# Row scaling by a diagonal matrix inside the transposes, and memory values computed token-major, in a one-core streaming encoder layer

## The chip, the cores and the metric

The kernel runs on one core of one Trainium2 chip. The metric is device time in microseconds (us). The core has TensorE (PE in the profile; PEld is its weight load), VectorE (DVE), ScalarE (ACT), GpSimd (POOL) and SyncE (SP), which here issues every DMA.

## The reference

One layer of an encoder, in float32, for 1024 prompt rows and 64 sample rows of width 1024. Only its beginning matters here:

```
h  = rmsnorm(x, g_pre)                 # x * rsqrt(mean(x*x) + eps) * g, row by row
... = split(h @ w_in)                  # 1024 -> 9216 columns: q, k, v, u, sv, mq, gates
kv = rmsnorm(mem, g_mem) @ w_mem_kv    # 256 memory tokens, 1024 -> 2048 columns
mem_k, mem_v = split(kv)               # each (256 tokens, 4 heads, 256); both are outputs
```

Then come stick-breaking attention, a spatial gating unit, attention over the memory, a gated merge, an output projection and a SwiGLU feed-forward, all fed by these products.

## The kernel before

**Precision and products.** A float32 operand is split into a high part (a cast to a reduced type, `Xh...`, `memh`, the first half of `whl`) and a low part (`Xl...`, `meml`: operand minus high part), and each product of the code (`mm3`, line 248) is three TensorE instructions: high by high, high by low, low by high.

**Memory stage.** The two 128-row memory tiles `mt` get their sum of squares on ScalarE (`rms_stage`, output `junk`), `rstd` from VectorE and GpSimd, a scaling by `rstd` in place (`scale_stage`), eight transposes of 128x128 each on TensorE (`tr4`, line 702, into the PSUM tiles `pt`, of which there are two), a scaling by the columns of g in the evacuation (`gain`, line 713: one VectorE instruction of 512 columns, or four ScalarE instructions of 128), and the split into `memh` and `meml`. Then `memkv_pair` (line 812) does w_mem_kv in eight pairs: for each of four heads 256 columns of k, then 256 of v. A pair loads two pieces `raw` of 512 KB, splits each into two `whl` (128x512), and multiplies: with each `whl` 12 TensorE instructions of 256 columns, called a chunk below, so 4 chunks a pair and 32 in all. The weights stand as the stationary operand, so the result has the output columns on its partitions (`mkT`, evacuated by ScalarE), and four transposes turn each pair back (`pt`, copied to `mko` by VectorE, stored).

**The x tiles.** Nine row tiles `xt` (eight of 128 rows, one of 64) go the same way: load, squares on ScalarE, `rstd`, scaling in place, `tr4`, `gain` into `bt`. `form_stages` (line 731) then makes the eight right-hand sides of a Strassen-type product from them: B11, B21, B22 are splits of `bt`; T2, T1, T3, T4 are sums and differences first, and then splits (f1 to f7). T2 and T1 need two subtractions on VectorE each, and one subtraction runs on GpSimd (`psub`).

**What sets the order.** The engines execute a fixed order, which the Python code writes out. It keeps its own model of each engine's clock (`Clocks`, line 93), and holds the x work as streams: lists of stages, each with the engine and a function that says when it is ready. Between and inside the chunks, `breathe` and `fill` take stages from the streams:

```
def breathe():
    tick()
    while clock["dve"] < clock["pe"] + BACK[0] and clock["act"] < clock["pe"] + BACK[0]:
        st = ready(0)
        if st is None:
            break
        go(st)
```

`ready` takes a stage whose operand is ready by the later of TensorE's and the stage's engine's modelled clock; BACK is 6 in the memory stage. `lighter` and `gain` choose between VectorE and ScalarE by these clocks. Nearly all instructions are recorded by one helper, line 83, so groups are told by tile names. After the memory stage the 36 Strassen units over w_in start, with `XhB11a` as the first right-hand side.

Of the kernel before, what the change touches and what calls it, by code (L numbers as in the profile page):

```python
# [9 lines left out]
F32 = mybir.dt.float32  # L10
F32R = mybir.dt.float32r
AF = mybir.ActivationFunctionType
ALU = mybir.AluOpType
AX = mybir.AxisListType

P = 128
T = 1088
HT = 544
D = 1024
# [73 lines left out]
class Clocks:  # L93
# [43 lines left out]
    def at(self, *tiles):  # L137
        return max([self.wrote.get(x.tensor.name, (0,))[0] for x in tiles], default=0) + self.LATENCY
# [16 lines left out]
def encoder_layer(  # L155
# [14 lines left out]
    clock, at = clocks.t, clocks.at  # L170
    nc = Engines(tc.nc, clocks)
# [3 lines left out]
    sm = ctx.enter_context(tc.tile_pool(name="sm", bufs=4))  # L175
# [6 lines left out]
    def nm(s):  # L182
        cnt[0] += 1
        return f"{s}_{cnt[0]}"

    def A(shape, dt=F32, s="a"):
        return arena.tile(shape, dt, tag="s", name=nm(s), bufs=NSLOT)

    def U(shape, dt=F32, s="u"):
        return arena.tile(shape, dt, tag="u", name=nm(s), bufs=NSMALL)  # L190
# [3 lines left out]
    def PB():  # L194
        t = ps.tile([P, 1024], F32, tag="b", name=nm("pb"), bufs=3)
        banks["b"] = banks["b"][-2:] + [t]
        return t
# [6 lines left out]
    def psum_free(tag, n=1):  # L204

        h = banks[tag]
        return clocks.done(h[n - 1]) if len(h) == (3 if tag == "b" else 2) else 0
# [3 lines left out]
    def f32(ap):  # L211
        return ap.bitcast(F32)
# [7 lines left out]
    def store(dst, src):  # L220
        nc.sync.dma_start(dst, src)

    def act(out, in_, f=AF.Copy, **kw):
        nc.scalar.activation(out, in_, f, **kw)
# [10 lines left out]
    def lighter(src, n, cost_dve):  # L235

        t = at(src)
        return max(clock["dve"], t) + cost_dve < max(clock["act"], t) + 0.1 + 0.00084 * n

    def split(src, hi, lo):  # L240
        n = math.prod(list(src.shape)[1:])
        if src.space == bass.MemoryType.SB and lighter(src, n, DVE_BIAS + 0.07 + 0.00057 * n):
            nc.vector.tensor_copy(hi, src)
        else:
            act(hi, src)
        sub(lo, src, f32(hi))

    def mm3(out, wh, wl, xh, xl, start, stop):
        nc.tensor.matmul(out, lhsT=wh, rhs=xh, start=start, stop=False)
        nc.tensor.matmul(out, lhsT=wh, rhs=xl, start=False, stop=False)  # L250
        nc.tensor.matmul(out, lhsT=wl, rhs=xh, start=False, stop=stop)

    def tp(out, in_):
        n = in_.shape[0]
        nc.tensor.transpose(out, in_, ident[:n, :n])


    ident = keep.tile([P, P], F32, tag="ident", name="ident")
# [13 lines left out]
    memk = [dtile([P, 1024], f"memk{h}") for h in range(4)]  # L272
    memv = [dtile([P, 1024], f"memv{h}") for h in range(4)]
# [24 lines left out]
    def later(n, fn, src=()):  # L298
        due.append((max([clock[e] for e in ("pe", "act", "dve")]) + 2.5 * n if n else at(*src), fn))
# [10 lines left out]
    def stream(*stages):  # L310
        st = list(stages)
        streams.append(st)
        return st
# [41 lines left out]
# [9 lines that stand above are left out]
    def fill(t):  # L364

        while clock["pe"] < t - 0.2:
            st = ready(t - 0.2)
# [3 lines that stand above are left out]
# [23 lines left out]
    def get_raw(i):  # L394
        return raw_t[i]
# [33 lines left out]
    def wop(fn, *rs):  # L429

        wops.append(fn)
        for r in rs:
            first_wop.setdefault(r, len(wops) - 1)
            last_wop[r] = len(wops) - 1
        return len(wops) - 1
# [12 lines left out]
    def raw_load(srcs, nk):  # L448

        def f():  # L450
            r = A([P, nk, 256], F32, "raw")
            w = 256 // len(srcs)
            for i, s in enumerate(srcs):
                load(r[:, :, i * w:(i + 1) * w], s.rearrange("(k p) m -> p k m", p=P))
            return r
        raws.append(f)
        return len(raws) - 1
# [216 lines left out]
    def rms_stage(x, d, junk=None):  # L674
# [7 lines left out]
            d["r"] = rstd_of(ss, D)  # L682
        return ("act", lambda: at(x()), sq)

    def scale_stage(get):

        def need():
            d = get()
            return None if d is None else at(d["r"])

        def sc():
            d = get()
            x, o = d["x"], d.pop("j")
            if lighter(x, D, 0.07 + 0.00057 * D):
                nc.vector.tensor_scalar(o, x, d["r"], None, op0=ALU.mult)
            else:
                act(o, x, scale=d["r"])
            d["x"] = o
            d["scaled"] = True
        return ("act", need, sc)  # L700

    def tr4(d):

        src = d["x"]
        n = src.shape[0]
        for h in range(2):
            pt = PT().rearrange("p (k q) -> p k q", k=4)
            for k in range(4):
                tp(pt[:, k, :n], src[:, (4 * h + k) * P:(4 * h + k + 1) * P])
            yield slice(4 * h, 4 * h + 4), pt[:, :, :n]  # L710
        d.clear()

# [96 lines left out]

    MH = {}  # L810

    def memkv_pair(h, kv):
        col = kv * D + h * 256
        parts = [([w_mem_kv[0, kh * 512:(kh + 1) * 512, col:col + 256]], 4) for kh in range(2)]
        st = {}

        def evac(m, hi, pt):
            if m == 0:
                st["t"] = U([P, 2, 256], F32, "mkT")
            act(st["t"][:, m, :], pt[:, :256])  # L820
            if m == 1:
                stream(("pe", lambda: max(at(st["t"]), psum_free("t")), fin))

        def fin():
            t = st["t"]
            pt = PT().rearrange("p (m d) -> p m d", m=2)
            for m in range(2):
                for dt in range(2):
                    tp(pt[:, m, dt * P:(dt + 1) * P], t[:, dt, m * P:(m + 1) * P])
            o = U([P, 2, 256], F32, "mko")  # L830
            nc.vector.tensor_copy(o, pt)
            dst = mem_v_prompt if kv else mem_k_prompt

            hl = A([P, 2, 2, 256], F32R, "mhl")
            split(o if kv else t, hl[:, 0], hl[:, 1])

            def put():
                store(dst[0, 0, :, h, :].rearrange("(m p) d -> p m d", p=P), o)
                store((memv if kv else memk)[h], f32(hl).rearrange("p s m d -> p (s m d)"))
            later(0, put, (o, hl))  # L840
        conv_pair(parts, lambda k, t, s: (MH["h"][k // 4][:, k % 4, :], MH["l"][k // 4][:, k % 4, :]),
                  [[(0, "a", cols_of(0, 256))]], evac)

    for h in range(4):
        for kv in range(2):
            memkv_pair(h, kv)
    n_mem = len(steps)


# [1196 lines left out]
    r = 0  # L2046
# [156 lines left out]
```

## Time and profile before

| | |
|---|---|
| median of 3 runs | 2277.43 us (2275.89 to 2277.76) |
| the profiled execution | 2276.9 us, of which its span 2275.2 us |
| PE busy | 2215.2 us, 97% of the span, 16465 matmul records |
| DVE busy | 1545.1 us, 68% |
| ACT busy | 756.6 us, 33% |
| mean granted TensorE clock | 0.994 |
| HBM read, written | 234.86 MB, 131.80 MB |

Shares over the whole span hide the beginning, in which the engines are loaded otherwise than later; the table by stretches below is read for that. A line of the timeline gives the start, the duration of the merged run of instructions, the engine, what is written and read, and in brackets how long the engine had been idle and what ended that. Consecutive instructions overlap in their pipelines, so the cost of one in a stream is the distance of two starts, which is less than its duration.

### The profile page before, as it was taken

The numbers are of one execution on the slowest core, as the hardware profiler recorded it, in microseconds if no ns is written. First come the engines' busy times: TensorE is split into PE (matmuls) and PEld (weight loads), VectorE is DVE, ScalarE is ACT, GpSimd is POOL, SyncE is SP. The second block draws the span as 40 slices with busy tenths as digits, with TensorE's granted clock in tenths as the row PEclk, the third lists the DMA queues.
The fourth block names the chain that finished last, engine by engine and source line by source line (L and its number), as shares of the span: only waits on it lengthen the run. The fifth ranks groups of instructions, "written<-read, shape, count | busy, mean of one in ns | idle before, by whom it ended". The sixth has DMA issues, their size and how long they took to land. (4 is left out here: it accounts for less than half of the span.)

```text
span 2275.2 us, 40734 instructions
## 1 busy us (share of the span) xinstructions
PE 2215.2 (97%) x16465; PEld 2141.9 (94%) x16465; DVE 1545.1 (68%) x2433; ACT 756.6 (33%) x1390; POOL 95.2 (4%) x172
## 2 busy tenths in 40 slices
PE   7899999999999999999999999997999999999998
PEld 6899999999999999889999999997999999998876
DVE  7955688865777776788734343458677677675677
ACT  8442222232212232566522021344112112124353
POOL 2000000000000000011000000121000000000000
PEclk9999999999999999999999999998999999999999
DMA  6523355775476658876835252132332233257235
GB/s 209 186 87 106 123 208 199 236 221 162 171 260 217 220 187 268 296 294 219 281 123 165 88 164 68 60 104 74 91 118 89 78 118 93 74 179 261 84 112 185
DMA packets 288367, 368.27 MB, mean 162 GB/s; under 512 B 20628, under 2 KB 220404, under 8 KB 288180
## 3 DMA queue, kind: packets, MB, share of 16 engines
q1 hardware_dynamic: 288180, 365.67, 48.6%
q8 instruction: 130, 2.13, 0.4%
q14 instruction: 57, 0.47, 0.1%
HBM read 234.86 MB, written 131.80 MB: 161 GB/s over the span
## 5 line engine op out<-in xcount | busy, mean ns | idle before, releaser
L83 ACT ACTIVATE whl<-raw 128x512 fp32r<-128x512 f32 x250 | 154.4, 633 | 519.8 <-PE pb L83 200.2
L83 DVE TENSOR_TENSOR c<-pb,u 128x544 f32<-128x544 f32 (+2 forms) x236 | 168.3, 713 | 230.4 <-PE pb L83 218.2
L83 PE MATMUL pb<-fop,fop 128*128 128x512 f32 x924 | 219.2, 390 | 1.9 <-DVE p L83 1.6
L83 PEld LDWEIGHTS pb<-fop,fop 128*128 128x128 f32 x924 | 173.0, 188 | 40.5 <-DVE p L83 2.4
L83 DVE TENSOR_TENSOR whl<-raw,whl 128x512 fp32r<-128x512 f32 x270 | 181.3, 686 | 12.5 <-ACT whl L83 11.8
L83 DVE TENSOR_TENSOR u<-pb,u 128x544 f32<-128x544 f32 (+2 forms) x177 | 125.7, 710 | 57.5 <-PE pb L83 56.6
L83 DVE TENSOR_TENSOR whl<-u,whl 128x512 fp32r<-128x512 f32 x232 | 160.1, 690 | 6.0
L83 PE MATMUL pb<-XhB11a,whl 128*128 128x288 f32 x592 | 130.8, 296 | 0.2 <-DVE whl L83 0.2
L83 PE MATMUL pb<-XhB21a,whl 128*128 128x288 f32 x592 | 130.8, 296 | 0.0
L83 PE MATMUL pb<-XhB22a,whl 128*128 128x288 f32 x592 | 130.3, 295 | 0.3 <-DVE whl L83 0.2
L83 PE MATMUL pb<-XhB11b,whl 128*128 128x256 f32 x592 | 119.8, 285 | 0.0
L83 ACT ACTIVATE c<-c 128x1088 f32<-128x1088 f32 x38 | 42.4, 1115 | 232.8 <-DVE c L83 232.8
L83 PE MATMUL pb<-XhB21b,whl 128*128 128x256 f32 x592 | 118.7, 283 | 0.0
L83 PE MATMUL pb<-XhB22b,whl 128*128 128x256 f32 x592 | 118.6, 283 | 0.0
L83 PE MATMUL pb<-XhT2a,whl 128*128 128x288 f32 x464 | 104.4, 300 | 2.7 <-DVE whl L83 0.6
L83 PE MATMUL pb<-XhT1a,whl 128*128 128x288 f32 x464 | 102.0, 295 | 1.0 <-DVE sgo L83 1.0
L83 PE MATMUL pb<-XhT3a,whl 128*128 128x288 f32 x464 | 102.2, 296 | 0.0
L83 PE MATMUL pb<-Xrh,whl 128*128 128x288 f32 (+1 forms) x512 | 100.0, 291 | 2.3 <-ACT ysq L83 2.3
L83 PE MATMUL pb<-XhT4a,whl 128*128 128x288 f32 x464 | 102.0, 295 | 0.0
L83 PEld LDWEIGHTS pb<-XhB22a,whl 128*128 128x128 f32 x592 | 99.0, 188 | 0.8 <-DVE whl L83 0.8
L83 PEld LDWEIGHTS pb<-XhB11a,whl 128*128 128x128 f32 x592 | 99.0, 188 | 0.7 <-DVE whl L83 0.4
L83 PEld LDWEIGHTS pb<-XhB21a,whl 128*128 128x128 f32 x592 | 99.0, 188 | 0.0
(330 smaller groups left out, 6247.4 us busy)
## 6 DMA issues: line engine op xcount, KB each, us to landing
raw<-in_w_in_dram SPq DMA_DIRECT2D x72, 512.0 KB
raw<-in_w_ffn_in_dram SPq DMA_DIRECT2D x88, 256.0 KB
gsc<-c SPq DMA_DIRECT2D x24, 544.0 KB
grow<-gsc SPq DMA_DIRECT2D x24, 544.0 KB
raw<-in_w_branch_dram SPq DMA_DIRECT2D x24, 512.0 KB
fS<-fsum SPq DMA_DIRECT2D x44, 256.0 KB
fw<-in_w_ffn_out_dram SPq DMA_DIRECT2D x44, 256.0 KB
fa<-fS SPq DMA_DIRECT2D x44, 256.0 KB
```

What stands on the lines that cost most here:

```text
L83: r = fn(*a, **k)
```

## The change

Two things. First, a tile that was to be scaled in place (the memory tiles and the nine x tiles; not the rows of the feed-forward, whose scaling has another target) is not scaled any more. Instead VectorE writes a 128x128 `diag` (the identity times `rstd`), and `tr4` multiplies the tile, as stationary operand, by it: an ordinary float32 product in the place of a transpose. At most three diags are open at a time. Second, the value half of `memkv_pair` becomes `memv_pair`: the memory tokens are the stationary operand and the weights the moving one, so that the result has tokens on its partitions and is evacuated to `mko` by ScalarE, without the transposes, `mkT` and the copy.

```
     def scale_stage(get):
         def need():
             d = get()
-            return None if d is None else at(d["r"])
+            return None if d is None or d["j"] is d["x"] and DIAG[0] == 3 else at(d["r"])
         def sc():
             d = get()
             x, o = d["x"], d.pop("j")
-            if lighter(x, D, 0.07 + 0.00057 * D):
+            if o is x:
+                DIAG[0] += 1
+                n = x.shape[0]
+                g = d["g"] = sm.tile([P, P], F32, tag="diag", name=nm("diag"), bufs=3)[:n, :n]
+                nc.vector.tensor_scalar(g, ident[:n, :n], d["r"], None, op0=ALU.mult)
+            elif lighter(x, D, 0.07 + 0.00057 * D):
                 nc.vector.tensor_scalar(o, x, d["r"], None, op0=ALU.mult)
...
             for k in range(4):
-                tp(pt[:, k, :n], src[:, (4 * h + k) * P:(4 * h + k + 1) * P])
+                a = src[:, (4 * h + k) * P:(4 * h + k + 1) * P]
+                if g is None:
+                    tp(pt[:, k, :n], a)
+                else:
+                    nc.tensor.matmul(pt[:, k, :n], lhsT=a, rhs=g, start=True, stop=True)
+            if g is not None and h == 1:
+                DIAG[0] -= 1
...
+    def memv_pair(h):
...
+            def f(tiles, kh=kh):
+                if kh == 0:
+                    fill(psum_free("b"))
+                    st["p"] = PB()
+                for q, w in enumerate(tiles):
+                    fill(at(w, MH["h"][kh], MH["l"][kh]))
+                    for m in range(2):
+                        for k in range(2):
+                            sl = (slice(None), 2 * q + k, slice(m * P, m * P + P))
+                            mm3(st["p"][:, m * 512:m * 512 + 256], MH["h"][kh][sl], MH["l"][kh][sl],
+                                w[:, 0, k], w[:, 1, k], kh == q == k == 0, kh == q == k == 1)
+                    breathe()
+                if kh == 1:
+                    st["o"] = U([P, 2, 256], F32, "mko")
+                    act(st["o"], st.pop("p").rearrange("p (m n) -> p m n", m=2)[:, :, :256])
+                    stream(("dve", lambda: at(st["o"]), fin))
+                    breathe()
```

Since the order comes out of the modelled clocks, it changes too, up to the first Strassen unit; from there on every engine's order is as before. Two places matter.

TensorE, from the last memory transposes (`mt`) to the x tiles (`xt`); `pb` is the accumulator of a pair. Before:

```order
L83 MATMUL pt_359<-ident,mt_299 128x128 x4
L83 MATMUL pb_388<-memh_314,whl_374 128x256
...
L83 MATMUL pb_388<-memh_315,whl_377 128x256
...
L83 MATMUL pb_455<-memh_314,whl_380 128x256
...
L83 MATMUL pb_455<-memh_315,whl_385 128x256
...
L83 MATMUL pt_493<-ident,xt_389 128x128 x4
L83 MATMUL pt_499<-ident,xt_389 128x128 x4
L83 MATMUL pb_491<-memh_314,whl_449 128x256
...
L83 MATMUL pt_554<-ident,xt_399 128x128 x4
```

And now:

```order
L83 MATMUL pt_361<-diag_332,mt_299 128x128 x4
L83 MATMUL pb_385<-memh_314,whl_373 128x256
...
L83 MATMUL pt_433<-diag_430,xt_386 128x128 x4
L83 MATMUL pt_439<-diag_430,xt_386 128x128 x4
L83 MATMUL pt_467<-diag_464,xt_394 128x128 x4
L83 MATMUL pt_473<-diag_464,xt_394 128x128 x4
L83 MATMUL pt_488<-diag_454,xt_402 128x128 x4
...
L83 MATMUL pt_626<-diag_623,xt_553 128x128 x4
L83 MATMUL pt_632<-diag_623,xt_553 128x128 x4
L83 MATMUL pb_385<-memh_315,whl_376 128x256
```

Before, the x tiles stood one by one between memory chunks, the first after four chunks; now all nine stand between the first chunk and the second.

VectorE, around the first x tiles (`diag` and `xt` are the scalings, `bt<-pt,cols` the evacuations by `gain`, `whl` the low parts of memory weights). Before:

```order
L83 TENSOR_SCALAR xt_389<-xt_389,rstd_394 128x1024
L83 CAST whl_449<-raw_372 128x512
L83 TENSOR_TENSOR whl_449<-raw_372,whl_449 128x512
L83 TENSOR_TENSOR whl_452<-raw_383,whl_452 128x512
L83 TENSOR_TENSOR whl_483<-raw_372,whl_483 128x512
L83 TENSOR_TENSOR whl_488<-raw_383,whl_488 128x512
L83 TENSOR_TENSOR bt_55_492<-pt_493,cols 128x512
L83 TENSOR_SCALAR rstd_526<-ss_59_523 64x1
L83 TENSOR_TENSOR XlB11a_530<-bt_55_492,XhB11a_529 128x4x128
```

And now:

```order
L83 TENSOR_SCALAR diag_430<-ident,rstd_391 128x128
L83 TENSOR_TENSOR bt_48_432<-pt_433,cols 128x512
L83 TENSOR_TENSOR bt_48_432<-pt_439,cols 128x512
L83 TENSOR_SCALAR rstd_451<-ss_52_448 64x1
L83 TENSOR_SCALAR diag_454<-ident,rstd_421 128x128
L83 CAST XhB11a_456<-bt_48_432 128x4x128
L83 TENSOR_TENSOR XlB11a_457<-bt_48_432,XhB11a_456 128x4x128
L83 TENSOR_TENSOR XlB21a_461<-bt_48_432,XhB21a_460 128x4x128
L83 TENSOR_SCALAR diag_464<-ident,rstd_399 128x128
L83 TENSOR_TENSOR bt_61_466<-pt_467,cols 128x512
L83 TENSOR_TENSOR bt_61_466<-pt_473,cols 128x512
```

Before, work on memory weights stood between the scaling of a tile and its evacuation; now the evacuation stands right behind its own diag, and every evacuation is on VectorE (33 of 512 columns in the program where there were 22, and 44 and 16 fewer on ScalarE).

Further down on VectorE, the formation of the T2 right-hand sides (`bt`, `t`, `XhT2b`, `XlT2b`) and the first memory weights after the x tiles, now:

```order
L83 TENSOR_TENSOR bt_93_568<-bt_105_606,bt_93_568 128x512
L83 TENSOR_TENSOR t_117_656<-bt_105_606,bt_93_568 128x512
L83 CAST XhT2b_658<-t_117_656 128x4x128
L83 TENSOR_TENSOR XlT2b_659<-t_117_656,XhT2b_658 128x4x128
L83 TENSOR_TENSOR whl_678<-raw_371,whl_678 128x512
L83 TENSOR_TENSOR whl_681<-raw_371,whl_681 128x512
```

The fifth chunk's weights (`whl_678`) stand behind all x evacuations and four T2 formations and the short one of the 64-row tile. On SP the nine x loads now stand ahead of all but three of the loads of memory weights; their number is unchanged.

## Rows read from the trace of the kernel before

**Rows 1.** Busy time by stretches (us from the span's start: length, then PE, PEld, DVE, ACT, POOL busy us with their instructions, the granted PE clock, the DMA share and GB/s).

```profile
40.00:50.00 10.00, 7.35 (x59) 6.80 (x59) 9.29 (x18) 10.00 (x35) 4.16 (x4) 1.00 0.37 107
50.00:60.00 10.00, 7.71 (x60) 6.87 (x60) 9.83 (x21) 9.54 (x26) 0.67 (x2) 1.00 0.08 20
80.00:90.00 10.00, 7.43 (x61) 7.16 (x60) 9.93 (x18) 5.58 (x12) 0.00 (x0) 1.00 0.93 323
95.00:110.00 15.00, 14.58 (x111) 14.12 (x112) 13.27 (x23) 4.33 (x8) 0.00 (x0) 1.00 0.55 193
110.00:300.00 190.00, 190.00 (x1519) 190.00 (x1518) 117.22 (x188) 58.38 (x87) 1.61 (x3) 1.00 0.36 116
```

**Rows 2.** The timeline of TensorE in the memory stage and at the first Strassen product; the ScalarE row is the evacuation of the four transposes that start at 63.71.

```profile
27.70 0.36 PE L83 MATMUL pb<-memh,whl 128*128 128x256 f32 x1
...
30.53 0.28 PE L83 MATMUL pb<-memh,whl 128*128 128x256 f32 x1
30.65 1.07 PE L83 MATMUL pt<-ident,xt 128*128 128x128 f32 x8
...
63.71 1.04 PE L83 MATMUL pt<-ident,xt 128*128 128x128 f32 x8
64.50 0.36 PE L83 MATMUL pb<-memh,whl 128*128 128x256 f32 x1
64.35 0.63 ACT L83 ACTIVATE bt<-pt,cols 128x128 f32<-128x128 f32 x2 [1.51 <-PE pt L83]
...
70.43 0.80 PE L83 MATMUL pb<-memh,whl 128*128 128x256 f32 x2 [2.95 <-DVE whl L83]
...
95.03 0.40 PE L83 MATMUL pb<-XhB11a,whl 128*128 128x288 f32 x1
```

**Rows 3.** The timeline of TensorE where the kernel before has ordinary float32 products of 128x128 (the spatial unit, 8 products in the code, 16 records), with the row that follows them.

```profile
642.64 1.95 PE L83 MATMUL pb<-wsT,vct 128*128 128x128 f32 x16
644.52 0.43 PE L83 MATMUL pt<-wsT,vct 64*128 64x64 f32 x2
```

**Rows 4.** The timeline of VectorE while it forms T2 (from 41.66) and T1 (from 45.15), a pair of `whl` (46.81), and the same for the 64-row tile (from 48.27).

```profile
41.66 0.68 DVE L83 TENSOR_TENSOR bt<-bt,bt 128x512 f32<-128x512 f32 x1
...
43.10 1.40 DVE L83 CAST XhT2a<-t 128x512 fp32r<-128x512 f32 x1
...
45.15 0.68 DVE L83 TENSOR_TENSOR bt<-bt,t 128x512 f32<-128x512 f32 x1
45.75 0.42 DVE L83 CAST XhT1a<-bt 128x512 fp32r<-128x512 f32 x1
...
46.81 1.28 DVE L83 TENSOR_TENSOR whl<-raw,whl 128x512 fp32r<-128x512 f32 x2
48.01 0.15 DVE L83 TENSOR_SCALAR rstd<-ss 128x1 f32<-128x1 f32 x1
...
48.27 0.29 DVE L83 TENSOR_TENSOR XlB21a<-bt,XhB21a 128x128 fp32r<-128x128 f32 x1
48.48 0.29 DVE L83 TENSOR_TENSOR bt<-bt,bt 128x128 f32<-128x128 f32 x1
...
50.73 0.68 DVE L83 TENSOR_TENSOR bt<-bt,t 128x512 f32<-128x512 f32 x1
```

**Rows 5.** The timeline of the first 24 us, TensorE, VectorE and ScalarE.

```profile
7.95 3.93 PE L83 MATMUL pt<-ident,mt 128*128 128x128 f32 x16
...
12.23 0.69 DVE L83 TENSOR_TENSOR bt<-pt,cols 128x512 f32<-128x512 f32 x1
...
13.63 2.17 ACT L83 ACTIVATE whl<-raw 128x512 fp32r<-128x512 f32 x4
...
21.04 1.05 ACT L83 ACTIVATE junk<-xt 128x1024 f32<-128x1024 f32 x1
...
22.29 0.75 DVE L83 TENSOR_SCALAR xt<-xt,rstd 128x1024 f32<-128x1024 f32 x1
...
23.10 1.10 PE L83 MATMUL pt<-ident,xt 128*128 128x128 f32 x8 [0.54 <-DVE xt L83]
```

**Rows 6.** Groups of equal instructions in the first 112 us (count, busy us, mean ns of one, idle time before them).

```profile
L83 DVE TENSOR_TENSOR bt<-pt,cols 128x512 f32<-128x512 f32 x9 | 6.1, 685 | 1.1 <-PE pt L83 1.1
L83 ACT ACTIVATE bt<-pt,cols 128x128 f32<-128x128 f32 x44 | 12.5, 416 | 2.6 <-PE pt L83 2.6
L83 ACT ACTIVATE xt<-xt,rstd 128x1024 f32<-128x1024 f32 x6 | 7.0, 1175 | 0.0
L83 ACT ACTIVATE mkT<-pb 128x256 f32<-128x256 f32 x16 | 6.6, 412 | 7.8 <-PE pb L83 7.8
L83 ACT ACTIVATE bt<-pt,cols 128x32 f32<-128x32 f32 x16 | 2.9, 330 | 0.0
L83 PE MATMUL pt<-ident,mkT 128*128 128x128 f32 x32 | 5.3, 292 | 0.0
```

**Rows 7.** Stretches by granted clock, with the columns of rows 1.

```profile
11.90:15.20 3.30, 0.50 (x2) 0.30 (x2) 3.23 (x6) 3.25 (x9) 0.00 (x0) 1.00 1.05 376
15.20:18.60 3.40, 3.24 (x15) 3.24 (x16) 2.07 (x5) 2.38 (x5) 0.49 (x1) 0.50 1.03 409
18.60:69.80 51.20, 41.71 (x331) 38.72 (x330) 44.39 (x84) 47.12 (x122) 10.73 (x13) 1.00 0.51 151
69.80:76.60 6.80, 6.17 (x29) 6.18 (x30) 6.63 (x10) 1.08 (x3) 1.76 (x1) 0.50 0.08 27
```

More of the change, by code (lines that the diff above doesn't have):

```diff
@@ L683, in rms_stage @@
         return ("act", lambda: at(x()), sq)
+    DIAG = [0]
     def scale_stage(get):
@@ L702, in tr4 @@
     def tr4(d):
-        src = d["x"]
+        src, g = d["x"], d.get("g")
         n = src.shape[0]
@@ L810, in encoder_layer, with memk_pair @@
     MH = {}
-    def memkv_pair(h, kv):
-        col = kv * D + h * 256
+    def memk_pair(h):
+        col = h * 256
         parts = [([w_mem_kv[0, kh * 512:(kh + 1) * 512, col:col + 256]], 4) for kh in range(2)]
@@ L831, in fin @@
             nc.vector.tensor_copy(o, pt)
-            dst = mem_v_prompt if kv else mem_k_prompt
             hl = A([P, 2, 2, 256], F32R, "mhl")
-            split(o if kv else t, hl[:, 0], hl[:, 1])
+            split(t, hl[:, 0], hl[:, 1])
             def put():
-                store(dst[0, 0, :, h, :].rearrange("(m p) d -> p m d", p=P), o)
-                store((memv if kv else memk)[h], f32(hl).rearrange("p s m d -> p (s m d)"))
+                store(mem_k_prompt[0, 0, :, h, :].rearrange("(m p) d -> p m d", p=P), o)
+                store(memk[h], f32(hl).rearrange("p s m d -> p (s m d)"))
             later(0, put, (o, hl))
@@ L842, in memkv_pair, with mk, wsplit2, fin @@
                   [[(0, "a", cols_of(0, 256))]], evac)
+    def memv_pair(h):
+        col = D + h * 256
+        st = {}
+        def mk(r, q):
+            return wop(lambda: wsplit2(get_raw(r)[:, 2 * q:2 * q + 2, :]), r)
+        def wsplit2(src):
+            t = A([P, 2, 2, 256], F32R, "whl")
+            split(src, t[:, 0], t[:, 1])
+            return t
+        def fin():
+            o = st["o"]
+            hl = A([P, 2, 2, 256], F32R, "mhl")
+            split(o, hl[:, 0], hl[:, 1])
+            def put():
+                store(mem_v_prompt[0, 0, :, h, :].rearrange("(m p) d -> p m d", p=P), o)
+                store(memv[h], f32(hl).rearrange("p s m d -> p (s m d)"))
+            later(0, put, (o, hl))
+        for kh in range(2):
+            r = raw_load([w_mem_kv[0, kh * 512:(kh + 1) * 512, col:col + 256]], 4)
+            ws = [mk(r, q) for q in range(2)]
+            def f(tiles, kh=kh):
[15 more added lines that the diff above has]
+                    breathe()
+            steps.append((ws, f))
     for h in range(4):
-        for kv in range(2):
-            memkv_pair(h, kv)
+        memk_pair(h)
+        memv_pair(h)
     n_mem = len(steps)
```

## The prediction

> **What bounds the kernel now.** I read the table by stretches first, because the shares of the whole span say only that TensorE is busy. From 110 us on TensorE is busy without a gap (190.00 of 190.00 us in the row from 110 to 300), and there its order is untouched, so what this change can give or take is the moment at which the Strassen units begin, and that moment shifts everything behind it [rows 1]. Before that moment TensorE waits: 7.35, 7.71 and 7.43 busy us in the stretches of 10 us from 40, 50 and 80 [rows 1]. VectorE is full there (9.29, 9.83, 9.93), ScalarE too until 60 (10.00, 9.54) and not after (5.58 from 80). The timeline gives the moment: the first Strassen product starts at 95.03, and the waits of TensorE ahead of it end with VectorE's `whl`, the longest with 2.95 us [rows 2]. So before 95 VectorE's row of work sets the pace, ScalarE shares it for the first 60 us, and TensorE has some slack. The question is when the first Strassen product starts in the new order.
>
> **What the change removes and adds.** ScalarE loses 44 evacuations of 128 columns (12.5 us) and 16 of 32 (2.9), six scalings (7.0), one of a memory tile, and half of the `mkT` (3.3 of 6.6); it gains four `mko` and three splits of 512 columns: some 23 us less [rows 6]. VectorE loses the scalings (four of about 0.7, from the row of 0.75) and four copies, and gains 11 evacuations of 512 columns (0.685 each, 0.60 from start to start), four small ones, 11 diags and five casts of weights, so it has about 4 us more, not less [rows 4 to 6]. A diag has no row; the same form over 1024 columns took 0.75 [rows 5] and instructions of 128 columns take 0.29 [rows 4], so it lies between 0.15 (a column) and 0.75, and I take 0.2 near the second, 0.15 from start to start. TensorE loses 16 transposes of `mkT` and turns 88 transposes into products. A transpose costs 0.10 (eight from 63.71 to 64.50) [rows 2]; an ordinary float32 product costs 1.88/8 = 0.235, since it is two records (642.64 to 644.52) [rows 3]. That is 12 us more for TensorE, against 1.6 us for the `mkT`. All three figures would matter little if the order had stayed. ScalarE's relief is worth nothing where ScalarE isn't waited for, and the order makes VectorE and TensorE wait for each other. I follow it in five steps to the first Strassen product.
>
> **Step 1, to the first x tile: 21.7.** The memory transposes start at 7.95 and took 3.93 for 16, 0.2 each, twice the 0.10 of later, so the engine is at its lower clock there [rows 2, 5]. The granted clock is full from 11.9 on [rows 7], so of the 16 products some eight cost 0.47 and the rest 0.235: 13.7, against 11.9 now. The last memory evacuation ends at 14.5 instead of 12.9 (12.23 and 0.69) [rows 5]. Behind it stand on ScalarE a `memh` (0.5), four `whl` (2.1) and four squares of x (1.05 each) [rows 5]: 21.4. The first x diag stands on VectorE behind the `rstd` of all four, so it comes at about 21.7, where the scaling now is at 22.29 [rows 5]. The removed scaling gains little, since the squares end last.
>
> **Step 2, the nine x tiles: 32 us.** VectorE has 46 instructions there: 16 evacuations, four small ones, two casts, eight low parts and two small ones, five `rstd`, nine diags, 18.5 us by 0.60, 0.2, 0.45, 0.60, 0.2, 0.07 and 0.15 from start to start, with a little for results that the next instruction reads [rows 4]. But seven of the diags stand directly ahead of their own tile's evacuation. From a diag to its evacuation it takes 0.06 to TensorE (23.04 to 23.10) [rows 5], four products of 0.235 [rows 3], what a record lasts beyond its 0.12 (0.17 of 0.29) [rows 6], and the release (0.1; four transposes that start at 63.71, 0.10 apart, release ScalarE at 64.35) [rows 2], 1.3 in all, and the second four products take 0.34 more than the first evacuation covers. That is 7 x 1.65 = 11.6 us of waiting on VectorE; the two tiles whose diag is ready earlier wait 0.6 and 1.4 for TensorE's pace. 18.5 and 13.6 are 32 us: the last x evacuation ends at 53.7. TensorE is busy for about half of this time, and can't take a memory chunk meanwhile, because all nine tiles stand ahead of the second chunk.
>
> The Trainium skill, "TensorE: Matmul & The Clock Gate", Terms, says that the transpose mode is four times faster for FP32. By that a product would cost 0.40 where rows 3 give 0.235, the waits would grow by some 11 us, and the sum below would end at 2314; I go by the trace's own products.
>
> **Step 3, the clock: 3.8 us.** After its first chunk TensorE has nothing until the first x diag, from about 18.3 (the chunk's weights come 2.5 behind the evacuation at 14.5) to 21.9. In the trace the gap of 2.95 us was followed by 6.8 us at half the granted clock (0.50, so 1.2 of 2.4 GHz), though TensorE was busy for 6.17 of them; the looser work before it kept the full clock, with 41.71 busy of 51.20 [rows 2, 7]. So I count the first two tiles at half clock: 8 x 0.235 more each, 3.8. The lower bound is none, the upper all nine tiles, 17 us.
>
> **Step 4, VectorE from there to the 19th chunk's weights: 43.4 us.** Behind the x evacuations stand 70 instructions up to that `whl`. T2 takes 3.49 a tile (41.66 to 45.15), since its cast takes 1.40 instead of 0.42 while GpSimd subtracts, and its short form 2.25 (48.48 to 50.73); T1 takes 1.66 (45.15 to 46.81) and its short form 0.7 [rows 4]. Four of each: 13.96, 2.25, 6.64, 0.7. Then 15 `whl`, 12 low parts and five memory copies and splits by 0.60, three small by 0.2: 19.8. TensorE's chunks 2 to 4 are done 4.3 us after the x tiles, and the fifth waits for 16 of these instructions of VectorE; a half clock here costs nothing, because VectorE is later anyway. In all, VectorE gets there at 21.7 + 32 + 3.8 + 43.4 = 100.9.
>
> **Step 5, TensorE from the 19th chunk: 20.9 us.** A chunk is 12 products of 0.12 (24 from 27.70 to 30.65, less the first), 1.44 [rows 2]. From here VectorE needs less than TensorE for a chunk (two `whl` and a cast or a copy for two chunks, 1.8 against 2.9), so TensorE is the bound: 14 chunks, 20.2, and two transposes of `mkT`, 0.7. The first Strassen product starts at 121.7, the sum of the five steps, against 95.03: 26.7 later. Some 0.75 comes back, because before a `mkT` transpose and short waits follow 95.03, seen in 14.58 busy of 15.00 us [rows 1]. So +25.9, on the profiled 2276.9: 2302.8; the median of before is 0.5 higher, so **2303**.
>
> The loads I cost at nothing: x now goes ahead of the memory weights on SP, VectorE and TensorE take tiles at 3.5 us each, and the DMA share is 0.37 from 40 and 0.08 from 50 already now [rows 1]. What is queued behind the waiting stores of `mko` and `mhl` on SP are raw pieces needed 2 to 6 us later; that cover is thin at the end, and a miss would add 2 us or so. The evacuation of `mko` on ScalarE is hidden by its idle time.
>
> **The rivals.** (a) VectorE does not wait in step 2, since the tiles overlap better than the order suggests: 13.6 and 3.8 less, 2285. Against it, no other x work stands between a diag and its evacuation. (b) TensorE stays at its lower clock for all of step 2, as its load there is about half and broken by gaps: 13 more than the forecast, 2316. For it speaks the stretch in which 6.17 of 6.8 us were busy and still at half clock; against it, that the full clock held through the loose stretch to 69.8, 41.71 of 51.20 [rows 7]. (c) Not slower: both the waits of (a) go, and GpSimd's subtractions, which now find T2 formations in a row, fall beside instructions that they don't slow, so that five casts take 0.42 and not 1.40: 4.9 less than (a), 2281, within 0.2%. For this speaks ScalarE's relief of 23 us, in the stretch in which it was full [rows 1, 6]. Against it speaks VectorE's own work: some 9.6 us ahead of the first x diag, 18.5 and 43.4, so that even from its first instruction near 6, without one wait and with those five casts short, it gets to the 19th chunk's weights at 72, and with step 5 the first Strassen product starts at 93, which is 2274 and still within 0.2%. A way to faster by over 0.2% I can't price; I leave it 0.04. (d) That the products aren't the two records of rows 3 but dearer: with the page's figure, 2314.
>
> **How the numbers follow.** Forecast 0.50 (2303, its own range 2295 to 2311 from an error of a quarter in the waits of step 2, and of 3.8 in step 3). (a) 0.15, (b) 0.17, (d) 0.05, (c) 0.09, all of it within 0.2%, and faster 0.04. The range takes in the forecast, (a), (b) and (d), 0.87 with some lost at the ends: 2285 to 2318. About 0.2%, 4.5 us, is what a measurement of this kernel can tell from no change; 2282 is its upper edge. So faster 0.04, same 0.09, slower 0.87.
>
> **What the profile of the changed kernel would show.** Step 1: the first `diag` product of x between 21 and 24. Step 2: VectorE idle ahead of `bt<-pt,cols`, released by PE `pt`, 10 us or more in sum, and the last x product near 56. Step 3: a granted clock of 0.5 in the first x tiles. Step 4: VectorE without gaps and TensorE idle some 10 us before the fifth chunk. Step 5: TensorE gapless from about 100, and `XhB11a` first near 122. The prediction is wrong if `XhB11a` comes before 105, or if the records of `pt<-diag,xt` are not two a product of about 0.12 each.

## The result, and the profile after

The changed kernel takes **2311.5 us** (median of 4 runs, 2310.4 to 2313.3) beside 2277.6 for the kernel before on the same chip (4 runs), a ratio of 1.0146 with a 95% interval of 1.0134 to 1.0158. That is 33.9 us more, where the prediction had 25.9 more (the quotient of the two medians is 1.0149, inside the interval). Two executions further below, one of before_raws_3 (3017.0 us) and one of gated_raws_3 (2409.7 us), ran at a lower clock and are left out of the medians. The profiled execution has a span of 2308.7 us, 33.5 more than before's 2275.2.

The timeline of TensorE after, from the first x tile to the first Strassen product; it answers to [rows 2, 5]:

```profile
22.48 3.75 PE L83 MATMUL pt<-diag,xt 128*128 128x128 f32 x16 [3.33 <-issue]
...
49.51 2.02 PE L83 MATMUL pt<-diag,xt 128*128 128x128 f32 x16 [1.02 <-issue]
...
58.01 2.55 PE L83 MATMUL pt<-diag,xt 128*128 128x128 f32 x16 [2.23 <-issue]
...
73.61 0.58 PE L83 MATMUL pb<-whl,memh 128*128 128x256 f32 x1 [6.59 <-DVE whl L83]
...
104.82 0.50 PE L83 MATMUL pb<-memh,whl 128*128 128x256 f32 x2 [0.67 <-DVE whl L83]
109.40 0.35 PE L83 MATMUL pb<-whl,memh 128*128 128x256 f32 x1 [1.69 <-DVE whl L83]
110.04 0.39 PE L83 MATMUL pb<-whl,memh 128*128 128x256 f32 x1 [0.28 <-DVE whl L83]
...
129.69 0.30 PE L83 MATMUL pb<-XhB11a,whl 128*128 128x288 f32 x1
```

The last row is the moment that counts: 129.69 instead of 95.03 [rows 2], 34.7 later, of which the span keeps 33.5. From 140 to 300 us TensorE is busy for 160.00 of 160.00 us (table below), as it was before from 110 on. The bracket `issue` at the x tiles means that the profile shows no releaser there; that their products wait for the diagonal is read from VectorE's times below.

Stretches by time after (columns as in [rows 1]), and below them stretches by granted clock:

```profile
20.00:30.00 10.00, 4.59 (x20) 4.35 (x21) 4.06 (x12) 5.76 (x11) 2.51 (x4) 0.50 0.57 173
50.00:60.00 10.00, 5.54 (x45) 5.22 (x44) 6.26 (x11) 1.26 (x2) 0.00 (x0) 0.97 0.00 0
80.00:90.00 10.00, 6.39 (x51) 5.98 (x50) 9.83 (x21) 5.58 (x12) 0.00 (x0) 1.00 0.48 158
140.00:300.00 160.00, 160.00 (x1281) 160.00 (x1281) 95.29 (x152) 48.83 (x74) 0.20 (x1) 1.00 0.30 96
...
18.40:32.00 13.60, 7.33 (x33) 6.80 (x33) 5.63 (x16) 7.36 (x15) 3.06 (x5) 0.50 0.53 155
32.00:38.90 6.90, 4.00 (x34) 3.75 (x33) 4.51 (x11) 2.71 (x5) 1.37 (x2) 0.99 0.47 154
38.90:49.10 10.20, 8.29 (x37) 7.61 (x35) 4.03 (x13) 1.25 (x3) 1.12 (x2) 0.50 0.16 52
```

In the x tiles no engine is full: VectorE is busy 4.06 of 10 us from 20 and 6.26 from 50, where before it had 9.29 and 9.83 between 40 and 60 [rows 1]; TensorE has 4.59 and 5.54. That all of them idle in part is what one sees when engines wait for each other in turn. The granted clock is half from 18.4 to 32.0 and from 38.9 to 49.1, and later again from 59.4 to 62.8, 69.6 to 79.8 and 110.6 to 114.0.

How they wait is seen on VectorE's timeline (the bracket is the idle time before an instruction and what ended it):

```profile
22.10 0.28 DVE L83 TENSOR_SCALAR diag<-ident,rstd 128x128 f32<-128x128 f32 x1
24.56 0.69 DVE L83 TENSOR_TENSOR bt<-pt,cols 128x512 f32<-128x512 f32 x1 [2.19 <-PE pt L83]
26.27 0.69 DVE L83 TENSOR_TENSOR bt<-pt,cols 128x512 f32<-128x512 f32 x1 [1.01 <-PE pt L83]
...
28.79 0.28 DVE L83 TENSOR_SCALAR diag<-ident,rstd 128x128 f32<-128x128 f32 x1
31.25 0.69 DVE L83 TENSOR_TENSOR bt<-pt,cols 128x512 f32<-128x512 f32 x1 [2.19 <-PE pt L83]
...
49.13 0.28 DVE L83 TENSOR_SCALAR diag<-ident,rstd 128x128 f32<-128x128 f32 x1
50.67 0.69 DVE L83 TENSOR_TENSOR bt<-pt,cols 128x512 f32<-128x512 f32 x1 [1.27 <-PE pt L83]
51.57 0.69 DVE L83 TENSOR_TENSOR bt<-pt,cols 128x512 f32<-128x512 f32 x1 [0.20 <-PE pt L83]
...
60.59 0.69 DVE L83 TENSOR_TENSOR bt<-pt,cols 128x512 f32<-128x512 f32 x1 [0.73 <-PE pt L83]
61.20 0.68 DVE L83 TENSOR_TENSOR bt<-bt,bt 128x512 f32<-128x512 f32 x1
...
68.16 0.28 DVE L83 TENSOR_TENSOR bt<-bt,bt 128x128 f32<-128x128 f32 x1
...
69.41 0.69 DVE L83 TENSOR_TENSOR bt<-bt,bt 128x512 f32<-128x512 f32 x1
...
96.45 1.29 DVE L83 TENSOR_TENSOR whl<-raw,whl 128x512 fp32r<-128x512 f32 x2 [1.07 <-ACT whl L83]
```

The diagonal is the instruction ahead of the wait, and the tile's products start 0.10 us behind its end (at 22.48 behind 22.10 and 0.28, at 49.51 behind 49.13 and 0.28). The waits of a tile's two evacuations are 1.27 and 0.20 us at full clock, 2.19 and mostly 1.01 at half. The group of these evacuations up to 95 us (count, busy us, mean ns of one, idle time before them):

```profile
L83 DVE TENSOR_TENSOR bt<-pt,cols 128x512 f32<-128x512 f32 (+1 forms) x24 | 14.7, 623 | 21.5 <-PE pt L83 21.3
```

The 24 evacuations waited 21.5 us in sum; in the kernel before, VectorE's evacuations waited 1.1 [rows 6].

### The profile page after: what moved, and what is told of

Read it like the earlier page. It is cut to its first block, busy times and chain, and to the rows that moved or that the text cites. A ratio compares the mean times of both kernels' runs of the same rounds, so it can differ in the third digit from the quotient of the medians.

```text
span 2308.7 us, 40828 instructions
## 1 busy us (share of the span) xinstructions
PE 2234.1 (97%) x16537; PEld 2163.3 (94%) x16537; DVE 1550.2 (67%) x2451; ACT 736.7 (32%) x1319; POOL 92.9 (4%) x172
## 5 line engine op out<-in xcount | busy, mean ns | idle before, releaser
L83 DVE TENSOR_TENSOR whl<-raw,whl 128x512 fp32r<-128x512 f32 x270 | 181.4, 686 | 11.9 <-ACT whl L83 11.1
```

What stands on the lines that cost most here:

```text
L83: r = fn(*a, **k)
```

## The experiments

The table has all twelve, in the order of the text below. "Over before" is the median less that of the kernel before on the same chip (2277.4 to 2278.0), in us, and what an edit is worth is worked out from this column. The last two are the start of the first Strassen product and VectorE's idle time ahead of evacuations (`bt<-pt,cols`) in the first 95 us, from the profiled execution.

| Kernel | Median us | Over before | Ratio to before (95%) | First Strassen | Waits |
|---|---|---|---|---|---|
| before | 2277.6 | 0 | 1 | 95.03 | 1.1 |
| after | 2311.5 | 33.9 | 1.0146 (1.0134 to 1.0158) | 129.69 | 21.5 |
| memv_only | 2277.2 | -0.2 | 0.9997 (0.9988 to 1.0007) | 97.04 | 1.7 |
| diag_only | 2310.6 | 33.2 | 1.0135 (1.0120 to 1.0151) | 129.18 | 23.3 |
| gated | 2286.4 | 8.9 | 1.0038 (1.0023 to 1.0052) | 105.33 | 5.9 |
| products_as_transposes | 2300.6 | 23.2 | 1.0094 (1.0079 to 1.0109) | 119.86 | 11.3 |
| gated_transposes | 2280.7 | 2.6 | 1.0012 (1.0002 to 1.0021) | 100.30 | 1.6 |
| diag_ahead | 2295.8 | 17.8 | 1.0079 (1.0064 to 1.0094) | 115.50 | 6.9 |
| keep_busy | 2306.4 | 28.4 | 1.0127 (1.0112 to 1.0142) | 123.27 | 16.2 |
| raws_3 | 2306.6 | 28.6 | 1.0126 (1.0110 to 1.0143) | 124.77 | 23.2 |
| before_raws_3 | 2278.3 | 0.6 | 0.9999 (0.9990 to 1.0008) | 95.39 | 1.1 |
| memv_raws_3 | 2278.1 | 0.3 | 1.0000 (0.9991 to 1.0009) | 96.61 | 1.1 |
| gated_raws_3 | 2282.0 | 4.2 | 1.0017 (1.0008 to 1.0026) | 100.52 | 2.5 |
| gated_early_raws_3 | 2282.7 | 5.0 | 1.0021 (1.0012 to 1.0030) | 100.79 | 2.4 |

The theory is the prediction's: the loss is the order, nine x tiles ahead of the second memory chunk, in which diagonal, products and evacuation of a tile run one after the other. The main rival is the price of the products themselves. First, which half of the change is it?

**memv_only.** The value half alone:

```diff
-    def memkv_pair(h, kv):      # of the kernel before
+    def memk_pair(h): ...       # of the changed kernel
+    def memv_pair(h): ...
     # scale_stage and tr4 of the kernel before: x scaled in place, plain transposes
```

> The value half of the change alone: memory values with memory tokens on the partitions (memk_pair and memv_pair as in the changed kernel), rows scaled ahead of plain transposes as before. In its order the x tiles stand one by one between memory chunks, as before. Theory (the loss is the nine x tiles ahead of the second chunk, which the diagonals bring about): no loss, 2272 to 2279, first Strassen product at 90 to 97 us, since TensorE saves 16 transposes (1.6 us) and VectorE four copies (some 2.4). Rival (the value half costs, through its evacuations on ScalarE and its splits on VectorE): 2285 or more.

No loss, and no gain either. The theory holds, but the four copies that VectorE was to save don't show: up to 95 us it is busy for 78.10 us where it was 77.47, because the planner gave it 13 evacuations instead of 9. TensorE's 16 saved transposes don't show either: its granted clock up to 95 us is 0.87 where it was 0.95, and how much of the gain went there wasn't tested.

**diag_only.** The other half alone, `scale_stage` and `tr4` of the changed kernel and `memkv_pair` of the kernel before:

> The diagonal half alone: x and memory rows scaled in products with a diagonal, memory keys and values both by the old pair. In its order all nine x tiles stand ahead of the second memory chunk, as in the changed kernel. Theory (the order behind the diagonals is the loss): nearly all of it, 2308 to 2316, first Strassen product at 127 to 134 us; slightly over the changed kernel, because the 16 transposes of the values are back. Rival (the value half makes half of the loss or more): 2295 or less.

33.2 us, all of the loss but 0.7, with waits as long. So the value half may be left aside.

**gated.** Now the order against the price. The planner holds an x tile's products ready when the rows of x are there, which is long before the diagonal is; this asks for both:

```diff
-  ... else max(at(x["x"]), psum_free("t"))
+  ... else max(at(x["x"], *([x["g"]] if "g" in x else [])), psum_free("t"))
```

> The whole change, but the planner's condition for an x tile's products also asks for its diagonal (at of d['g'] as well as of the rows). The same products, the same diagonals and the same values; in its order the x tiles stand one by one between memory chunks again, and 48 of the x evacuations of 128 columns are on ScalarE instead of 16. Theory (order): the loss goes, 2272 to 2284, no wait of VectorE for a tile's own products over 0.5 us on average, and full clock through the x tiles. Rival (the price of the products, 12 us of TensorE and more at half clock, is the loss): 2295 or more.

One condition in the planner takes back 25.0 of 33.9 us, with the same products and diagonals. It moves evacuations too: up to 95 us VectorE has 16 of them where the changed kernel has 24 (9.4 us busy for 14.7), so the 25.0 is the worth of the order together with this choice; diag_ahead below moves nothing but the diagonals. The theory's main point holds, but the time is 2.4 over its range and the clock was not full. The timeline of TensorE in this kernel:

```profile
35.66 1.95 PE L83 MATMUL pt<-diag,xt 128*128 128x128 f32 x16
...
41.00 0.50 PE L83 MATMUL pb<-memh,whl 128*128 128x256 f32 x2 [2.19 <-DVE whl L83]
...
42.38 3.59 PE L83 MATMUL pt<-diag,xt 64*128 64x64 f32 x16
```

Its rows of the table by stretches from 40 us:

```profile
40.00:50.00 10.00, 9.00 (x47) 8.75 (x48) 6.33 (x17) 5.51 (x16) 1.35 (x2) 0.66 0.09 29
50.00:60.00 10.00, 9.66 (x81) 9.27 (x79) 8.64 (x17) 6.71 (x19) 2.23 (x2) 1.00 0.75 239
```

Between the tiles there is memory work again, and most tiles take 1.95 us for 16 records. TensorE is busy for 9.00 of 10 us from 40, in part at half clock, and for 9.66 at full clock from 50, where it had 7.71 before [rows 1]. It is now the engine with little slack there, so its products can be expected to have a price; gated_transposes below measures it.

**products_as_transposes.** The price in the changed kernel's own order:

```diff
-  nc.tensor.matmul(pt[:, k, :n], lhsT=a, rhs=g, start=True, stop=True)
+  nc.tensor.engine.transpose(pt[:, k, :n], a, g)          # g is made of ones
+  clocks.account("pe", "matmul", [pt[:, k, :n]], [a, g])  # the planner sees a product
```

> The changed kernel's order on every engine, but each product with the diagonal is a transpose (the matrix that it is given is the diagonal turned into ones, made on VectorE by an instruction of the same shape and waited for as before). The scaling of the rows is left out. Theory (order: diagonal, product and evacuation one behind the other): the chain stays and only its products shrink, 0.235 to 0.10 each, so some 6 to 10 us less, 2301 to 2306, and VectorE still waits 8 us or more ahead of the x evacuations. Rival (the price of the products is the loss): 2290 or less.

10.7 us less, 0.4 under the theory's range, and still 23.2 over the kernel before; VectorE still waits 11.3 us, so the chain stays. TensorE's timeline in this kernel:

```profile
45.15 1.94 PE L721 MATMUL pt<-diag,xt 128*128 128x128 f32 x8 [2.23 <-issue]
```

And the stretch of the x tiles (columns as in [rows 1]):

```profile
22.00:50.00 28.00, 15.21 (x68) 12.20 (x67) 18.46 (x43) 8.81 (x18) 3.36 (x6) 1.00 0.28 84
```

A tile's eight transposes take 1.94 us here, 0.24 each from end to end, as the memory transposes did at half clock (16 in 3.93) [rows 5], although the column says 1.00. So they cost half as much as the products at half clock (3.75 a tile), but as much as products at full clock (1.95). The edit took away about what the half clock adds to the products, and not their price at equal clock; the next run measures that.

**gated_transposes.** The same edit in the order of gated.

> The order of gated on every engine, with transposes in place of the products with the diagonal (the diagonal turned into ones, waited for as before); the scaling of the rows is left out. Gated is 9 us over the kernel before. Theory (what is left there is the price of the products: 88 of them at 0.235 instead of 0.10, 12 us of TensorE, and the half clock that they meet): most of it goes, 2276 to 2280. Rival (what is left is VectorE, with 16 evacuations of x where it had 9, and late weights): 2283 to 2287.

2280.7, 0.7 over the theory's range: the products' price in this order is 8.9 less 2.6, 6.3 us, about half of 88 x 0.135 = 11.9, which it would be if TensorE had no slack at all. The clock isn't what differs: from 22 to 62 us it is 0.91 in gated and 0.87 here. Here the eight transposes of a tile take what they took before [rows 2]:

```profile
22.74 1.03 PE L721 MATMUL pt<-diag,xt 128*128 128x128 f32 x8
```

**diag_ahead.** The chain by itself: the same order everywhere, but each diagonal issued one to three tiles earlier on VectorE, the planner's clocks left as they were.

```diff
+  def pump():     # called at scale_stage and after each tile's last product
+      while WAIT and LIVE[0] < 3 and DONE[0] < 11:
+          ...     # next tile in the order of the products, if its rstd is made
+          d["g"] = sm.tile([P, P], F32, tag="diag", name=nm("diag"), bufs=3)[:n, :n]
+          nc.vector.engine.tensor_scalar(d["g"], ident[:n, :n], d["r"], None, op0=ALU.mult)
```

> The changed kernel's order on TensorE, ScalarE, GpSimd and SP, and VectorE's order but for the nine diagonals of x, which are issued one to three tiles ahead of their products (still three buffers) instead of directly ahead of their own tile's evacuation. Nothing else is changed. Theory (the diagonal stands behind the evacuations of the tile before, so diagonal, product and evacuation of each tile run one after the other): VectorE's waits ahead of the x evacuations fall from 21 us to 6 to 12, TensorE's pace being what is left, the x tiles end 9 to 15 us earlier, and the time is 2297 to 2303. Rival (TensorE's products set the pace there, wherever the diagonals stand): 2307 or more.

Moving nine small instructions takes 16.1 us away, 1.2 more than the theory's range allowed. VectorE's timeline now shows three diagonals in a row and evacuations with short waits or none:

```profile
22.48 0.67 DVE L705 TENSOR_SCALAR diag<-ident,rstd 128x128 f32<-128x128 f32 x3
24.94 0.69 DVE L83 TENSOR_TENSOR bt<-pt,cols 128x512 f32<-128x512 f32 x1 [1.80 <-PE pt L83]
26.70 0.29 DVE L705 TENSOR_SCALAR diag<-ident,rstd 128x128 f32<-128x128 f32 x1 [1.07 <-PE pt L83]
...
29.22 0.68 DVE L83 TENSOR_TENSOR bt<-pt,cols 128x512 f32<-128x512 f32 x1
29.82 0.24 DVE L705 TENSOR_SCALAR diag<-ident,rstd 64x64 f32<-64x64 f32 x1
29.98 0.68 DVE L83 TENSOR_TENSOR bt<-pt,cols 128x512 f32<-128x512 f32 x1
```

The waits ahead of evacuations fall from 21.5 to 6.9. Four diagonals now wait for TensorE's products instead (1.07 at 26.70 is the longest), 2.6 us in sum. The x tiles end 12.5 us earlier (the first T2 starts at 48.71 instead of 61.20), and the first Strassen product comes 14.2 us earlier. The rival, that TensorE's products set the pace there, falls. The clock rises along with it, from 22 to 62 us in the changed kernel and here:

```profile
22.00:62.00 40.00, 26.91 (x152) 25.46 (x153) 20.97 (x49) 9.61 (x18) 3.93 (x7) 0.71 0.22 65
22.00:62.00 40.00, 27.83 (x189) 26.21 (x190) 32.26 (x66) 14.42 (x29) 9.35 (x10) 0.84 0.25 67
```

So the 16.1 us is the serialisation together with the part of the half clock that goes with it.

**keep_busy.** The clock: three products more ahead of each full tile's own, into the same bank, which don't wait for the diagonal.

```diff
+  for k in range(3):   # first half of each 128-row x tile
+      nc.tensor.engine.matmul(pt[:, k, :n], lhsT=src[:, k * P:(k + 1) * P],
+                              rhs=ident[:n, :n], start=True, stop=True)
```

> The changed kernel with three more float32 products ahead of each full x tile's own, with the unit matrix as their right-hand side, which doesn't wait for the diagonal, into the bank that the tile's own products then overwrite: work for TensorE in the time in which it waits for the diagonal. It adds 24 products, 5.6 us at full clock, nearly all of it in that waiting time. Theory (TensorE falls to half clock there since it waits so much): the granted clock stays at or near 1.00 from 22 to 62 us, each tile's own products take 1.9 instead of 3.75 us, and the time is 2303 to 2310 though there is more work. Rival (the clock falls for another reason, so that more products bring more half clock or as much): clock 0.75 or less in that stretch and 2312 or more.

TensorE does more work and the kernel is 5.5 us shorter. Its stretches:

```profile
18.00:30.00 12.00, 8.30 (x40) 7.71 (x40) 5.16 (x15) 7.67 (x15) 3.05 (x5) 0.58 0.63 184
30.00:56.00 26.00, 20.71 (x166) 19.17 (x165) 16.19 (x37) 5.84 (x11) 2.48 (x4) 1.00 0.19 62
```

From 30 us on the clock is full where it was half in parts; the first tile still ran at half. So the half clock from the second tile on costs the changed kernel about 5 us, and in this run work in TensorE's idle time kept it away. The theory's time holds (2306.4), its clock only after the first 8 us.

**raws_3.** The end of the stage. In the changed kernel VectorE waits for a piece of the weights that SP issued behind stores (SPq is SP's queue):

```profile
106.00 0.34 SPq L83 DMA_DIRECT2D memv<-mhl  x1
106.43 2.00 SPq L83 DMA_DIRECT2D raw<-in_w_mem_kv_dram  x2
...
108.83 0.43 DVE L83 CAST whl<-raw 128x512 fp32r<-128x512 f32 x1 [2.86 <-DMA raw<-in_w_mem_kv_dram]
```

```diff
-    RA[0] = 2
+    RA[0] = 3
     LA[0] = LA_MEM
```

> The changed kernel with the raw pieces of the memory weights loaded one chunk of weights earlier (RA 3 instead of 2 in the memory stage); three high parts change between ScalarE and VectorE. In the changed kernel two casts waited for such a piece, 2.86 us at 108.8 and 2.48 at 125.1, behind stores on SP. Theory (these waits lie on the path): they go, and the time is 2306 to 2310. Rival (TensorE has other waits in their place): 2311 to 2313.

5.3 us less, though its runs spread more (2303 to 2310). The stretch from the 19th chunk to the first Strassen product took 24.9 us in the changed kernel, with 2 us of idle time and a granted clock of 0.93:

```profile
104.80:129.70 24.90, 22.91 (x175) 22.54 (x176) 16.19 (x29) 7.84 (x15) 0.00 (x0) 0.93 0.89 291
```

In raws_3 it takes 21.6, at full clock:

```profile
103.20:124.80 21.60, 21.38 (x175) 21.02 (x176) 16.01 (x29) 7.65 (x15) 0.00 (x0) 1.00 0.96 322
```

Its 19th chunk also starts 1.6 earlier, at 103.20: the first diagonal stands behind two `rstd` instead of four and comes at 20.22, and high parts have changed engines, so this much isn't the loads' doing.

**Is any version faster than the kernel before?** The last four take the earlier loads: before_raws_3 and memv_raws_3 with nothing else, gated_raws_3 with the gate, and gated_early_raws_3 with the gate and each diagonal as a stream of its own. Their expectations follow the edit in this order:

```diff
+    for i in (0, 1, 2, 3, 8, 4, 5, 6, 7):
+        stream(scale_stage(lambda i=i: N.get(i)))
     for j in (0, 1, 4, 2, 3):
-        stream(*form_stages(j, ..., c_gpre))
+        stream(*form_stages(j, ..., c_gpre, sc=False))   # no scale_stage inside
```

> The kernel before with the raw pieces of the memory weights loaded one chunk of weights earlier (RA 3 instead of 2 in the memory stage), as a base for the next three. In the kernel before, ScalarE waits 2.3 us in sum for such pieces up to 95 us. Theory (VectorE's row of work sets the pace there, and the loads are hidden but for a little): 2275 to 2278. Rival (the late pieces are on the path): 2272 or less.

> The value half alone with the loads of before_raws_3; in its order the x tiles stand between the memory chunks. Theory (the value half takes 1.6 us from TensorE and some 2.4 from VectorE; memv_only lost that again to waits for weights, 1.9 us of them for raw pieces, and to half clock): 2272 to 2276, a little under the kernel before. Rival (the value half is worth nothing): 2276 to 2278, as memv_only.

> The whole change with the planner's condition of gated and the loads of before_raws_3; x tiles one by one between memory chunks, 28 evacuations of x and memory rows on VectorE. Theory (in gated, ScalarE waited 4.8 us for raw pieces and VectorE 1.4, part of it on the path, and the products' price of 6 us stays): 2280 to 2285. Rival (the loads cost the whole 9 us): 2277 or less.

> As gated_raws_3, with the diagonals as streams of their own, so that they are issued ahead of the evacuations of the tile before, as in diag_ahead. Theory (with no wait for a diagonal what is left is the price of the products, some 6 us): 2278 to 2283, not below the kernel before. Rival (ScalarE's and VectorE's relief by the missing scalings shows once the order and the loads are right): 2272 or less.

None is. The loads are worth nothing in the kernel before, and 4.7 us with the gate (8.9 to 4.2). The value half is worth nothing with them either: the theory missed here, its rival holds. Once order and loads are right, the change costs some 4 us, and issuing the diagonals earlier takes nothing off that (5.0 and 4.2). That these 4 us are the products' price fits gated_transposes, but transposes with the earlier loads weren't run.

## Why the prediction was right, and where its sizes were off

The time lies inside the range of 2285 to 2318 and the order of events was as forecast, but the sum was 8.0 us short (33.9 for 25.9), and the time lies 0.5 us over the forecast's own range of 2295 to 2311, between the forecast and rival (b). By its own steps, up to the first Strassen product:

| Step | Forecast us | Measured us | From |
|---|---|---|---|
| 1, to the first x diagonal | 21.7 | 22.1 | 22.10 |
| 2 and 3, the nine x tiles | 32 + 3.8 | 39.1 | 22.10 to 61.20 |
| 4, VectorE to the 19th chunk | 43.4 | 43.6 | 61.20 to 104.82 |
| 5, TensorE to `XhB11a` | 20.9 | 24.9 | 104.82 to 129.69 |
| sum | 121.7 (121.8 from the rounded terms) | 129.7 | 129.69 |

**Steps 1 and 4** hold within half a microsecond, step 4 in part by luck. Four T2 casts are long as described (1.37 to 1.40), but the short T2 takes 1.25 (68.16 to 69.41) where 2.25 was taken from before, and a wait of 1.07 at 96.45, which the forecast didn't have, makes up for that. Ahead of the fifth chunk stand three T2 formations and the short one, the 16 instructions of step 4, and not four and the short one. TensorE's gap there is 6.59 where some 10 were forecast.

**Steps 2 and 3** were 3.3 short. The waits, with the clock's part, were 17.4 by the forecast and are 18.8 (the 21.3 of the group that end with TensorE's `pt`, less 2.5 ahead of 22 us, for the memory tiles): 1.47 a tile at full clock where 1.65 was forecast, but some five of nine tiles met half clock where two were counted. The other 1.8 is VectorE's own work, 20.3 for 18.5. Most of it comes from counting the distance of two starts for instructions that stand ahead of a wait, where the whole duration counts: seven diagonals at 0.28 for 0.15 and eight evacuations at 0.69 for 0.60, 1.6 in all. diag_ahead shows that the waits hang on the diagonals' place, and keep_busy that the clock's part is more than 3.8: about 5 us go with the half clock from the second tile on, and the first tile, at half clock there too, waits for 3.20 (2.19 and 1.01) instead of 1.47. The products are two records of 0.12 at full clock (16 in 1.95), so rival (d) falls. The Trainium skill, "TensorE: Matmul & The Clock Gate", Terms, has the transpose mode four times faster for FP32. Here a product costs 0.235 and a transpose 0.10 [rows 2, 3] at the same clock, a factor of about 2.4, and the measurement decides.

**Step 5** is the step that failed, in its cost of the loads: "I cost at nothing", with "2 us or so" for a miss. A miss (the cast's 2.86, of which TensorE idled 1.69 and 0.28) and the half clock that followed it make up the 4.0 but for some 0.3; with the loads earlier the same stretch takes 21.6, within 0.7 of the forecast.

Of the rivals, (a) and (c) are excluded by the waits of 21.5 us, and (b) was half right: the half clock held for more than the first tiles, not for all. The reading that TensorE's waits before 95 us end with VectorE's `whl` leaves out six in the trace of before, up to 52 us, that end with ScalarE's `bt`, 3.6 us in sum. That the price "would matter little if the order had stayed" was too strong: with the order mended by the gate it is 6.3 us, with TensorE busy for 9.66 of 10 us from 50.

So of the 33.9 us the order, with its waits, its half clock and its choice of engines, accounts for 25.0 (gated). The other 8.9 go to the products (6.3 by gated_transposes) and late loads (4.7 by gated_raws_3); these two were measured apart, the second in an order that differs a little, so they overlap and are no strict sum.

## What to carry to other kernels

Where a program orders the work by modelled times, look at what a new operand does to the condition for "ready": here the products waited for a diagonal that the condition didn't know, and with the condition mended the nine tiles no longer stand ahead of the other work (25.0 us). An instruction that feeds another engine should stand one tile ahead of the work that drains that engine: nine diagonals moved took 16.1 us away. Where other work already stood between the tiles, a like move gave nothing (gated_early_raws_3). When the busy shares of all engines fall together, look first for two that wait for each other in turn.

## What the runs showed of the hardware

- In products_as_transposes the transposes of x took 0.24 us each (1.94 for 8 from end to end) until the memory chunks at 51 us, and in gated_transposes and the kernel before, between memory chunks, 0.13 (1.03 for 8). The granted clock reads 1.00 for both. Where a trace shows no change of the clock yet, the column says little; the duration of equal instructions says more.
- The memory tiles at the start show the same difference. In the changed kernel their 32 records, from 7.80, took 5.64 us, which is 16 at 0.235 and 16 at 0.12: the clock rose among them. The 16 transposes of products_as_transposes, from 7.68, took 3.82, and the x tiles behind them stayed as slow. The Trainium skill, "TensorE: Matmul & The Clock Gate", Part 4, says that the full clock doesn't engage for transposes. That run agrees, but the kernel before doesn't: behind its 16 transposes (from 7.95 to 11.88) [rows 5] the granted clock is 1.00 from 11.9 on [rows 7], and the first product behind them takes 0.38, as at full clock, where it takes 0.58 in products_as_transposes. What makes the difference stays open.
- More work on TensorE made the kernel faster (keep_busy, by 5.5 us): from 30 to 56 us its clock was 1.00, where the changed kernel had 0.76.

The memory tiles in the changed kernel, then those of products_as_transposes with the first product behind them, then that product in the kernel before:

```profile
7.80 5.64 PE L83 MATMUL pt<-diag,mt 128*128 128x128 f32 x32
...
7.68 3.82 PE L721 MATMUL pt<-diag,mt 128*128 128x128 f32 x16
14.42 0.58 PE L83 MATMUL pb<-memh,whl 128*128 128x256 f32 x1 [2.92 <-ACT whl L83]
...
14.30 0.38 PE L83 MATMUL pb<-memh,whl 128*128 128x256 f32 x1 [2.41 <-ACT whl L83]
```
